# MLP up-projection of column groups 2 to 7 as Strassen 2x2 block products

## Chip, cores and metric

One core of one Trainium2 chip. The metric is the device time of one execution in microseconds (us); the kernel before takes 691.36 us, the median of three runs (689.93 to 691.77).

## What is computed

Two decoder layers on x of 256 rows by 1024 columns in float32: layer 0 is retention, layer 1 MoBA attention, each followed by a squared-ReLU MLP. What matters here is the MLP, twice:

```
h = relu(x @ w_up)          # [256, 1024] @ [1024, 4096]
y = (h * h) @ w_down        # [256, 4096] @ [4096, 1024]
```

## The kernel before

Every float32 product is made of three float32r matmuls on two parts of each operand: hi*hi, hi*lo and lo*hi (`mm`, lines 176 to 181). The activations are held transposed in two parts (class `HT`: `hi` and `lo`, eight k tiles of 128 by 256 rows). Rows come in two row tiles t of 128, the 4096 hidden columns in eight groups g of 512.

**The weight stream.** Class `Stream` (lines 90 to 160) brings all weights in chunks of 128 x 1024 in the order of use. `load` issues one chunk's DMA on the SP queue into one of four `raw` buffers; `split` makes its two parts: ScalarE copies it, rounded, into `whi` (line 134), and VectorE takes the difference into `wlo` (line 135). Ten pairs of parts can be live. `get` hands the next chunk to a product; if none is split yet, it splits one at that place in the program. An up-projection chunk is two k tiles of one group of 512 columns; a down-projection chunk is one k tile of 1024 columns.

**What sets the order.** There is no scheduler at run time: each engine carries out its instructions in the order in which the Python code emits them. Class `Flow` keeps a model time `now` that the matmuls advance. After each product step `advance` lets side chains (generators that yield a delay) go on, and calls `pump`, which emits a split when a slot is free and `next_t` has been reached. After a split, `next_t` is moved on by 1.3 or 2.0 model us.

**The MLP** (`mlp`, from line 396). Groups 0 and 1 are computed by `in_groups_skewed` with the activations stationary; `act_rows` squares them and transposes them on TensorE. For each group g from 2 to 7, `up_cols` takes four chunks and makes the transposed result at once, weights stationary: four 128-column tiles, eight k tiles, three matmuls of 256 columns each, into two PSUM tiles `upc`. `act_cols` then runs Relu on ScalarE (line 417), the square on VectorE (line 419) and the split into the parts of `hid[g]` (lines 197 and 198). Behind each group four k steps of the down projection follow (`step_out`; hidden group g-2), each twelve matmuls of 512 columns into `dn`. In the last layer the second half of row tile 1's accumulator is two tiles of 256 columns (line 452). The last eight k steps are done by `finish_out` or `finish_last`.

Of the kernel before, what the change touches and what calls it, by code (L numbers as in the profile page):

```python
# [17 lines left out]
P = 128  # L18
# [66 lines left out]
class Chunk:  # L85
    def __init__(self, hi, lo):
        self.hi, self.lo, self.left = hi, lo, CH * S


class Stream:  # L90
    """Weight chunks in the order of use: loaded, then split into two float32r parts."""

    def __init__(self, tc, ctx, flow, slots, raws):
# [3 lines left out]
        self.src, self.raw, self.ready = [], [], []  # L97
        self.live, self.next_t, self.dma_t = 0, 0.0, 0.0
        flow.pump = self.pump

    def load(self):
        """issue the next chunk's load, and the other loads that come before it"""
        while self.src:
            s = self.src.pop(0)
            self.dma_t = max(self.dma_t, self.flow.now + 1.6)
            if callable(s):
                s()
                self.dma_t += 1.0
                continue
# [10 lines left out]
            return  # L120

    def split(self, pres=(None,)):
        nc = self.nc
        if not self.raw:
            self.load()
        raw = self.raw.pop(0)[0]
# [10 lines left out]
        self.ready.append(Chunk(hi, lo))  # L137
        self.next_t = max(self.next_t, self.flow.now) + (1.3 if len(self.ready) < 4 else 2.0)
        while len(self.raw) < self.raws and self.src:
            self.load()  # L140

    def pump(self):
        while self.live < self.slots and self.flow.now >= self.next_t:
            if not self.raw:
                self.load()
            if not self.raw or self.flow.now < self.raw[0][1]:
                return
            self.split()
# [14 lines left out]
def body(ctx, tc, xT, x, gT, gpost, w_in_0, w_out_0, w_up_0, w_down_0, w_in_1, w_out_1, w_up_1, w_down_1,  # L163
# [12 lines left out]
    def mm(o, a, b, first, last):  # L176
        """o += a.T @ b; a, b: (hi, lo) pairs of float32r parts."""
        nc.tensor.matmul(o, a[0], b[0], start=first, stop=False)  # L178
        nc.tensor.matmul(o, a[0], b[1], start=False, stop=False)  # L179
        nc.tensor.matmul(o, a[1], b[0], start=False, stop=last)  # L180
        flow.now += 3 * b[0].shape[-1] / 2400
# [766 lines left out]
```

## Time and profile before

| | |
|---|---|
| runs, median (lowest to highest) | 691.36 us (689.93 to 691.77) |
| profiled execution, span from first to last instruction | 688.4 us |
| its own time outside the span | not listed; the runs' median is 3.0 us above the span |
| TensorE matmuls (PE) busy | 676.1 us, 98% |
| VectorE (DVE) busy | 419.4 us, 61% |
| ScalarE (ACT) busy | 350.4 us, 51% |
| DMA | 125.09 MB, 182 GB/s in the mean |

Busy time of PE is the time covered by matmuls, whose ends are modelled and overlap the next one's start. So the pace of TensorE is read from the distance between two starts, not from the duration of one. For DVE and ACT both exist: the duration of one instruction, which counts where another engine waits for its end, and the distance between two starts on the same engine, which counts in an unbroken sequence. A releaser ("<-") is what ended an idle time.

### The profile page before, as it was taken

How to read it: one execution, taken by the hardware profiler on the slowest of the kernel's cores; microseconds unless marked ns; L12 is line 12 of the kernel's file. 1: busy time of each engine (PE TensorE's matmuls, PEld its weight loads, DVE VectorE, ACT ScalarE, POOL GpSimd, SP SyncE). 2: the span in 40 equal slices, each digit the busy share in tenths (PEclk: the TensorE clock that was granted, in tenths of full speed). 3: DMA queues.
4: the chain of work that ended last, by engine and by line, in shares of the span. 5: the costliest groups of instructions: out<-in, count | busy, mean ns of one | idle time of the engine just before them, and what ended most of it. 6: DMA issues, size and time to landing. Idle time of an engine off the chain costs nothing. (4 is left out here: it accounts for less than half of the span.)

```text
span 688.4 us, 10014 instructions
## 1 busy us (share of the span) xinstructions
PE 676.1 (98%) x3919; PEld 594.3 (86%) x3919; DVE 419.4 (61%) x521; ACT 350.4 (51%) x493; POOL 82.2 (12%) x138
## 2 busy tenths in 40 slices
PE   8999999999999999999999999999999999999996
PEld 6889898988888988998898878888889999999985
DVE  5669576656458665545653867867686654465513
ACT  6475555445346545435542657755465554345411
POOL 0222120201001000000000263922010000000001
PEclk9999999999999999999999999999999999999998
DMA  7767565464624774457545456543246744674401
GB/s 274 284 208 267 200 212 177 155 206 154 241 93 157 241 251 169 157 190 244 176 140 175 169 184 219 184 148 123 83 161 235 258 155 151 211 231 148 164 9 62
DMA packets 36191, 125.09 MB, mean 182 GB/s; under 512 B 4272, under 2 KB 4784, under 8 KB 36144
## 3 DMA queue, kind: packets, MB, share of 16 engines
q1 hardware_dynamic: 36144, 124.45, 53.0%
q8 instruction: 31, 0.51, 0.3%
q14 instruction: 16, 0.13, 0.1%
HBM read 123.39 MB, written 1.05 MB: 181 GB/s over the span
## 5 line engine op out<-in xcount | busy, mean ns | idle before, releaser
L135 DVE TENSOR_TENSOR wlo<-raw,whi 128x1024 fp32r<-128x1024 f32 (+1 forms) x227 | 271.5, 1212 | 114.1 <-ACT whi L134 112.8
L134 ACT ACTIVATE whi<-raw 128x1024 fp32r<-128x1024 f32 (+1 forms) x227 | 231.1, 1042 | 86.9 <-DMA raw<-in_w_down 21.1
L178 PE MATMUL ip<-whi,act 128*128 128x512 f32 x288 | 114.2, 397 | 0.0
L179 PE MATMUL ip<-wlo,act 128*128 128x512 f32 x288 | 112.5, 391 | 0.2 <-DVE wlo L135 0.2
L180 PE MATMUL ip<-whi,act 128*128 128x512 f32 x288 | 112.4, 390 | 0.0
L178 PE MATMUL upc<-act,whi 128*128 128x256 f32 x384 | 108.8, 283 | 0.0
L180 PE MATMUL upc<-act,wlo 128*128 128x256 f32 x384 | 108.7, 283 | 0.0
L179 PE MATMUL upc<-act,whi 128*128 128x256 f32 x384 | 108.7, 283 | 0.0
L179 PE MATMUL dn<-wlo,act 128*128 128x512 f32 (+1 forms) x288 | 105.6, 367 | 0.0
L178 PE MATMUL dn<-whi,act 128*128 128x512 f32 (+1 forms) x288 | 105.6, 367 | 0.0
L180 PE MATMUL dn<-whi,act 128*128 128x512 f32 (+1 forms) x288 | 105.3, 366 | 0.0
L178 PEld LDWEIGHTS upc<-act,whi 128*128 128x128 f32 x384 | 73.7, 192 | 0.3
L179 PEld LDWEIGHTS upc<-act,whi 128*128 128x128 f32 x384 | 73.7, 192 | 0.3
L180 PEld LDWEIGHTS upc<-act,wlo 128*128 128x128 f32 x384 | 73.7, 192 | 0.0
L180 PEld LDWEIGHTS ip<-whi,act 128*128 128x128 f32 x288 | 54.1, 188 | 11.6
L179 PEld LDWEIGHTS ip<-wlo,act 128*128 128x128 f32 x288 | 54.2, 188 | 10.7 <-DVE wlo L135 0.7
L178 PEld LDWEIGHTS ip<-whi,act 128*128 128x128 f32 x288 | 54.2, 188 | 10.0
L178 PEld LDWEIGHTS dn<-whi,act 128*128 128x128 f32 x288 | 54.4, 189 | 8.9
L180 PEld LDWEIGHTS dn<-whi,act 128*128 128x128 f32 x288 | 54.2, 188 | 8.9
L179 PEld LDWEIGHTS dn<-wlo,act 128*128 128x128 f32 x288 | 54.4, 189 | 8.6
L310 POOL TENSOR_TENSOR po_c<-po_sum,mhalf 128x1 f32<-128x1 f32 x8 | 4.5, 563 | 379.4 <-DVE po_sum L298 379.4
L417 ACT ACTIVATE r<-upc 128x512 f32<-128x512 f32 x24 | 14.3, 597 | 60.8 <-PE upc L180 60.8
(156 smaller groups left out, 862.4 us busy)
## 6 DMA issues: line engine op xcount, KB each, us to landing
raw<-in_w_in SPq DMA_DIRECT2D x69, 512.0 KB, 3.9
raw<-in_w_up SPq DMA_DIRECT2D x64, 512.0 KB, 4.5
raw<-in_w_down SPq DMA_DIRECT2D x64, 512.0 KB, 4.1
raw<-in_w_out SPq DMA_DIRECT2D x24, 512.0 KB, 3.3
gb<-in_gpost SPq DMA_DIRECT2D x4, 512.0 KB, 5.4
raw<-in_w_in SPq DMA_DIRECT2D x6, 256.0 KB, 5.6
h<-in_x SPq DMA_DIRECT2D x2, 512.0 KB, 6.6
dT_sb<-in_dT SPq DMA_DIRECT2D x4, 256.0 KB, 4.8
```

The source lines that it names most:

```text
L134: nc.scalar.activation(hi[:, c], raw[:, c], AF.Copy)
L135: nc.vector.tensor_sub(lo[:, c], raw[:, c], hi[:, c].bitcast(F32))
L178: nc.tensor.matmul(o, a[0], b[0], start=first, stop=False)
L179: nc.tensor.matmul(o, a[0], b[1], start=False, stop=False)
L180: nc.tensor.matmul(o, a[1], b[0], start=False, stop=last)
L310: nc.gpsimd.tensor_tensor(c, self.ss, mhalf, ALU.pow)
L417: nc.scalar.activation(r, o, AF.Relu)
```

## The change

Groups 2 to 7 are taken in three blocks of two groups (g, g+1). A block's product is a 2x2 block product: the activations in quarters by row tile and by even and odd k tiles, the weights in quarters by even and odd k tiles and by group (`_blocks` on the host reorders `w_up` accordingly). Seven products of quarters, Winograd's form of Strassen's scheme, take the place of eight. `product` makes one: four k tiles, three matmuls each, activations stationary, 512 columns, two chunks of weights.

The activation sums (`hsum`) are made once per MLP by `block_sums`. Four of the seven products of a block need sums of weight quarters: the quarters are loaded into four tiles `quad` (128 x 2 x 1024), and `Stream.split` adds one to another in place on VectorE before it splits the sum. The results are put together from PSUM by VectorE (`u2`, `u3`, `c`); Relu and the square run on ScalarE (`squared`); as the result is not transposed now, `turned` transposes it on TensorE and splits it. `down()` is one k step of the down projection; eight of them stand between and behind a block's products. `pump` waits also for the model's landing time of the quarters, and a split costs 1.3 to 2.3 model us. The last layer's accumulator is no longer divided into 256 columns.

```diff
+    def loaded(self):
+        op = self.order[0]
+        if op is None:
+            return self.raw[0][1] if self.raw else None
+        t = [self.landed.get(n) for n in op.needs]
+        return None if None in t else max(t)
...
+        while self.loaded() is None:
+            assert self.load()
+        op = self.order.pop(0)
         hi = self.pool.tile([P, CH], F32R, tag="whi", name="whi", bufs=self.slots)
         lo = self.pool.tile([P, CH], F32R, tag="wlo", name="wlo", bufs=self.slots)
+        full = len(self.ready) >= 4
+        if op is None:
+            raw = self.raw.pop(0)[0]
+            cost = 2.0 if full else 1.3
+        else:
+            raw = self.quads[op.q][:, op.half, :]
+            cost = 1.7 if full else 1.3
+            if op.add is not None:
+                nc.vector.tensor_add(raw, raw, self.quads[op.add][:, op.half, :])
+                cost += 0.6 if full else 1.0
...
             nc.scalar.activation(hi[:, c], raw[:, c], AF.Copy)
             nc.vector.tensor_sub(lo[:, c], raw[:, c], hi[:, c].bitcast(F32))
         self.live += 1
-        self.ready.append(Chunk(hi, lo))
-        self.next_t = max(self.next_t, self.flow.now) + (1.3 if len(self.ready) < 4 else 2.0)
-        while len(self.raw) < self.raws and self.src:
-            self.load()
+        self.quad_ops += op is not None
+        self.ready.append(Chunk(hi, lo, CH * S if op is None else CH * P))
+        self.next_t = max(self.next_t, self.flow.now) + cost
+        while len(self.raw) < self.raws and self.load():
+            pass
...
-        def act_cols(g, jp, o):
-            r = new_e2([P, 2, S], "r")
-            nc.scalar.activation(r, o, AF.Relu)
-            sq = new_e2([P, 2, S], "sq")
-            nc.vector.tensor_mul(sq, r, r)
+        def turned(g, t, c):
+            yield 1.6
+            tp = new_ps([P, 4, P], "tp_u")
+            turn4(tp, c)
+            ts = slice(t * P, (t + 1) * P)
+            split(hid[g][:, 0, :, ts], hid[g][:, 1, :, ts], tp)
+        def squared(g, t, o, add=None, sign=1.0):
+            c = new_e2([P, 512], "c")
+            if add is None:
+                nc.scalar.activation(c, o, AF.Relu, scale=sign)
+            else:
+                nc.vector.tensor_add(c, o, add)
+                nc.scalar.activation(c, c, AF.Relu, scale=sign)
+            nc.scalar.activation(c, c, AF.Square)
+            done[g].append(flow.spawn(turned(g, t, c)))
+        s_hi, s_lo = [p.tile([P, 4, 4, P], F32R, name=n, tag="act" if p is act else n)
+                      for p, n in ((act, "s_hi"), (qpool, "s_lo"))]
+        def block_sums():
+            (a11, a12), (a21, a22) = [[hg[:, t, e::2, :] for e in range(2)] for t in range(NT)]
+            f = [new_e2([P, 4, P], "hsum") for _ in range(4)]
+            nc.vector.tensor_sub(f[0], a22, a21)
             yield 0.8
+            nc.vector.scalar_tensor_tensor(f[1], f[0], -1.0, a11, op0=ALU.mult, op1=ALU.subtract)
+            split(s_hi[:, 0], s_lo[:, 0], f[0])
+            yield 1.6
+            nc.vector.tensor_sub(f[2], a11, a21)
+            split(s_hi[:, 1], s_lo[:, 1], f[1])
+            yield 1.6
+            nc.vector.scalar_tensor_tensor(f[3], f[1], -1.0, a12, op0=ALU.mult, op1=ALU.subtract)
+            split(s_hi[:, 2], s_lo[:, 2], f[2])
+            yield 1.6
+            split(s_hi[:, 3], s_lo[:, 3], f[3])
...
-        def up_cols(g):
-            chunks = [ws.get() for _ in range(4)]
-            for jp in range(2):
-                o = new_ps([P, 2, S], "upc")
-                for j in range(2):
-                    f0 = (jp * 2 + j) * P
-                    for k in range(KD):
-                        s = slice((k % 2) * 512 + f0, (k % 2) * 512 + f0 + P)
-                        mm_cols(o[:, j, :], chunks[k // 2], s, hT.both(k), k == 0, k == KD - 1)
-                done[g].append(flow.spawn(act_cols(g, jp, o)))
+        def quad(t, e):
+            return lambda kp: hT.tile(2 * kp + e, t)
+        def hsum(i):
+            return lambda kp: (s_hi[:, i, kp, :], s_lo[:, i, kp, :])
+        def product(o, lhsT, first):
+            for half in range(2):
+                w = ws.get()
+                for kk in range(2):
+                    kp = 2 * half + kk
+                    mm_rows(o, lhsT(kp), w, slice(kk * 512, (kk + 1) * 512), first and kp == 0, kp == 3,
+                            not first)
+        def up_blocks(g, down):
+            x = new_ps([P, 512], "px")
+            product(x, quad(0, 0), True)
+            p1 = new_e2([P, 512], "p1")
+            nc.scalar.activation(p1, x, AF.Copy)
+            down()
+            z = new_ps([P, 512], "pz")
+            product(z, hsum(0), True)
+            down()
+            y = new_ps([P, 512], "py")
+            product(y, hsum(1), True)
+            u2 = new_e2([P, 512], "u2")
+            nc.vector.tensor_add(u2, y, p1)
+            down()
+            product(y, hsum(2), False)
+            u3 = new_e2([P, 512], "u3")
+            nc.vector.tensor_add(u3, y, p1)
+            squared(g + 1, 1, z, u3, -1.0)
+            down()
+            product(x, quad(0, 1), False)
+            squared(g, 0, x)
+            down()
+            product(y, quad(1, 1), False)
+            squared(g, 1, y, p1)
+            down()
+            product(z, hsum(3), False)
+            squared(g + 1, 0, z, u2, -1.0)
+            down()
+            down()
...
+        sums = flow.spawn(block_sums())
-        if nxt is None:
-            acc[1] = [acc[1][0], acc[1][1][:, :256], new_ps([P, 256], "dn4")]
         nk = FF // P
-        for g in range(2, NG):
+        ks = iter(range(nk - SKEW))
+        def down():
+            k, w = next(ks), ws.get()
+            for t in range(NT):
+                step_out(acc, lhs, k, t, w, nk)
+        for g in range(2, NG, 2):
+            new_hid(g + 1)
             new_hid(g)
-            up_cols(g)
-            for k in range((g - 2) * 4, (g - 1) * 4):
-                w = ws.get()
-                for t in range(NT):
-                    step_out(acc, lhs, k, t, w, nk)
+            flow.finish(sums)
+            up_blocks(g, down)
+        ws.quads = None
...
+            gates = (0, 0, 0, 0) if b == 0 else (last + 8, last + 12, last + 12, last + 14)
+            at = (8 * b - 1, 8 * b + 1, 8 * b + 1, 8 * b + 2) if b else (0, 0, 0, 1)
+            for i in range(4):
+                for half in range(2):
+                    q = QuadLoad(place[i], half, up[c0 + 2 * i + half], gates[i], (b, i, half))
+                    due.setdefault(at[i], []).append(q)
+            q1, q2, q3, q4 = place
+            ops = [(q1, None, (0,)), (q1, q2, (0, 1)), (q1, q3, (0, 2)), (q2, q3, (1, 2)), (q4, None, (3,)),
+                   (q1, q4, (0, 3)), (q3, None, (2,))]
+            for j, (q, add, needs) in enumerate(ops):
+                ws.order += [QuadOp(q, add, half, [(b, i, half) for i in needs]) for half in range(2)]
+                ws.order += [None] * (1 if j < 6 else 2)
+            place = [q2, q4, q1, q3]
```

Here is VectorE's queue in block 2 of the first MLP (groups 4 and 5), and the corresponding place before (group 4). `raw` is a chunk of `w_down`, `quad0` to `quad3` are the weight quarters, `py`, `pz` and `px` the products in PSUM, `tp_u` the transposed squares, `act` is `hid`. Before:

```order
L135 TENSOR_TENSOR wlo_2711<-raw_2631,whi_2710 128x1024
L135 TENSOR_TENSOR wlo_2738<-raw_2649,whi_2737 128x1024
L419 TENSOR_TENSOR sq_2748<-r_2746 128x512
L198 TENSOR_TENSOR act_2678<-sq_2748,act_2678 128x512
L135 TENSOR_TENSOR wlo_2784<-raw_2667,whi_2783 128x1024
L419 TENSOR_TENSOR sq_2809<-r_2807 128x512
L135 TENSOR_TENSOR wlo_2815<-raw_2687,whi_2814 128x1024
L198 TENSOR_TENSOR act_2678<-sq_2809,act_2678 128x512
```

Now:

```order
L177 TENSOR_TENSOR quad1_2030<-quad1_2030,quad0_2029 128x1024
L185 TENSOR_TENSOR wlo_2703<-quad1_2030,whi_2702 128x1024
L535 TENSOR_TENSOR u2_2713<-py_2695,p1_2640 128x512
L185 TENSOR_TENSOR wlo_2716<-raw_2557,whi_2715 128x1024
L177 TENSOR_TENSOR quad3_2032<-quad3_2032,quad0_2029 128x1024
L185 TENSOR_TENSOR wlo_2734<-quad3_2032,whi_2733 128x1024
L177 TENSOR_TENSOR quad3_2032<-quad3_2032,quad0_2029 128x1024
L185 TENSOR_TENSOR wlo_2745<-quad3_2032,whi_2744 128x1024
L539 TENSOR_TENSOR u3_2755<-py_2695,p1_2640 128x512
L481 TENSOR_TENSOR c_2757<-pz_2659,u3_2755 128x512
L185 TENSOR_TENSOR wlo_2762<-raw_2576,whi_2761 128x1024
L250 TENSOR_TENSOR act_2614<-tp_u_2778,act_2614 128x4x128
```

A sum and its difference now stand next to each other; u2 reads the product whose last chunk is split in the row just ahead of it; the next chunk's split stands behind u2. The row on `tp_u` reads the transposed form of the `c` two rows above it.

ScalarE's queue at the same place. Before:

```order
L134 ACTIVATE whi_2737<-raw_2649 128x1024
L417 ACTIVATE r_2746<-upc_2679 128x512
L197 ACTIVATE act_2678<-sq_2748 128x512
L134 ACTIVATE whi_2783<-raw_2667 128x1024
L417 ACTIVATE r_2807<-upc_2750 128x512
```

Now:

```order
L184 ACTIVATE whi_2744<-quad3_2032 128x1024
L482 ACTIVATE c_2757<-c_2757 128x512
L483 ACTIVATE c_2757<-c_2757 128x512
L184 ACTIVATE whi_2761<-raw_2576 128x1024
L249 ACTIVATE act_2614<-tp_u_2778 128x4x128
L184 ACTIVATE whi_2788<-quad2_2031 128x1024
L184 ACTIVATE whi_2798<-quad2_2031 128x1024
L479 ACTIVATE c_2808<-px_2616 128x512
L483 ACTIVATE c_2808<-c_2808 128x512
L184 ACTIVATE whi_2811<-raw_2624 128x1024
```

The next down chunk (`whi_2761`, later `whi_2811`) stands behind the Relu and the square of the product just ended.

TensorE's queue behind u3, where that down chunk is used. Before, behind an up-projection group, the `dn` matmuls followed without a transposition:

```order
L180 MATMUL upc_2750<-act_1667,wlo_2608 128x256
L178 MATMUL dn_2252<-whi_2627,act_2256 128x512
L179 MATMUL dn_2252<-wlo_2628,act_2256 128x512
L180 MATMUL dn_2252<-whi_2627,act_2256 128x512
L178 MATMUL dn_2253<-whi_2627,act_2256 128x512
```

Now:

```order
L230 MATMUL dn_2261<-whi_2761,act_2264 128x512
L231 MATMUL dn_2261<-wlo_2762,act_2264 128x512
L232 MATMUL dn_2261<-whi_2761,act_2264 128x512
L254 MATMUL tp_u_2778<-ident_96,c_2757 128x128 x4
L230 MATMUL dn_2262<-whi_2761,act_2264 128x512
L231 MATMUL dn_2262<-wlo_2762,act_2264 128x512
L232 MATMUL dn_2262<-whi_2761,act_2264 128x512
L230 MATMUL px_2616<-whi_2788,act_1668 128x512
```

The four transpositions of `c` stand behind nine of the twelve `dn` matmuls of the chunk `whi_2761`.

## Rows read from the trace of the kernel before

**Rows 1.** Busy time by engine, whole span.

```profile
PE 676.1 (98%) x3919; PEld 594.3 (86%) x3919; DVE 419.4 (61%) x521; ACT 350.4 (51%) x493; POOL 82.2 (12%) x138
```

**Rows 2.** Windows: two middle groups; groups 2 to 7. Stretch, length; busy PE, PEld, DVE, ACT, POOL; clock; DMA.

```profile
275.30:320.20 44.90, 44.90 (x290) 41.11 (x289) 24.58 (x25) 20.88 (x24) 0.00 (x0) 1.00 0.57 187
230.40:365.20 134.80, 134.80 (x869) 123.48 (x868) 77.21 (x78) 65.52 (x77) 0.00 (x0) 1.00 0.60 197
```

**Rows 3.** Timeline of PE, group 2's up and down projection; start, duration.

```profile
230.39 0.28 PE L178 MATMUL upc<-act,whi 128*128 128x256 f32 x1
230.50 0.28 PE L179 MATMUL upc<-act,whi 128*128 128x256 f32 x1
230.62 0.28 PE L180 MATMUL upc<-act,wlo 128*128 128x256 f32 x1
...
242.34 0.40 PE L178 MATMUL dn<-whi,act 128*128 128x512 f32 x1
242.57 0.40 PE L179 MATMUL dn<-wlo,act 128*128 128x512 f32 x1
...
253.25 0.28 PE L178 MATMUL upc<-act,whi 128*128 128x256 f32 x1
```

**Rows 4.** Timeline of PE, one transposition of four tiles in group 1.

```profile
228.56 0.60 PE L202 MATMUL tp_u<-ident,sq 128*128 128x128 f32 x4
228.91 0.48 PE L178 MATMUL ip<-whi,act 128*128 128x512 f32 x1
229.23 0.39 PE L179 MATMUL ip<-wlo,act 128*128 128x512 f32 x1
```

**Rows 5.** Groups of instructions by form, DVE and ACT: count, busy us, mean ns, idle before.

```profile
L135 DVE TENSOR_TENSOR wlo<-raw,whi 128x1024 fp32r<-128x1024 f32 x221 | 267.6, 1226 | 113.4 <-ACT whi L134 112.1
L134 ACT ACTIVATE whi<-raw 128x1024 fp32r<-128x1024 f32 x221 | 227.6, 1054 | 86.5 <-DMA raw<-in_w_down 21.1 <-PE upc L179 15.4 <-DMA raw<-in_w_up 15.4
L417 ACT ACTIVATE r<-upc 128x512 f32<-128x512 f32 x24 | 14.3, 597 | 60.8 <-PE upc L180 60.8
L197 ACT ACTIVATE act<-sq 128x512 fp32r<-128x512 f32 x24 | 15.0, 624 | 10.4 <-DVE sq L419 10.4
L198 DVE TENSOR_TENSOR act<-tp_u,act 128x512 fp32r<-128x512 f32 x8 | 5.5, 690 | 8.7 <-ACT act L197 8.5
L197 ACT ACTIVATE act<-tp_u 128x512 fp32r<-128x512 f32 x8 | 4.8, 599 | 16.5 <-PE tp_u L202 16.5
```

**Rows 6.** Timeline of DVE: an unbroken sequence at the end of the first out projection.

```profile
202.45 1.22 DVE L135 TENSOR_TENSOR wlo<-raw,whi 128x1024 fp32r<-128x1024 f32 x1
203.59 1.29 DVE L198 TENSOR_TENSOR act<-hg,act 128x512 fp32r<-128x512 f32 x2
204.79 1.22 DVE L135 TENSOR_TENSOR wlo<-raw,whi 128x1024 fp32r<-128x1024 f32 x1
```

**Rows 7.** Timeline of ACT behind the last `upc` matmul of group 2.

```profile
242.60 0.60 ACT L417 ACTIVATE r<-upc 128x512 f32<-128x512 f32 x1 [1.28 <-PE upc L180]
243.09 1.05 ACT L134 ACTIVATE whi<-raw 128x1024 fp32r<-128x1024 f32 x1
244.04 0.61 ACT L197 ACTIVATE act<-sq 128x512 fp32r<-128x512 f32 x1
```

**Rows 8.** Timeline: the last `upc` matmul of group 2, then a handover chain in group 3.

```profile
242.22 0.28 PE L180 MATMUL upc<-act,wlo 128*128 128x256 f32 x1
...
259.20 0.60 ACT L417 ACTIVATE r<-upc 128x512 f32<-128x512 f32 x1 [4.58 <-PE upc L180]
259.83 0.69 DVE L419 TENSOR_TENSOR sq<-r 128x512 f32<-128x512 f32 x1 [3.95 <-ACT r L417]
260.55 0.63 ACT L197 ACTIVATE act<-sq 128x512 fp32r<-128x512 f32 x1 [0.76 <-DVE sq L419]
```

**Rows 9.** Windows at the kernel's start; columns as in rows 2, granted clock third from the right.

```profile
5.50:8.90 3.40, 2.08 (x10) 1.47 (x11) 1.87 (x3) 1.68 (x4) 0.00 (x0) 1.00 0.96 327
8.90:12.30 3.40, 3.40 (x19) 3.40 (x18) 3.37 (x7) 3.36 (x7) 0.00 (x0) 0.51 1.05 395
12.30:15.70 3.40, 3.40 (x30) 3.40 (x30) 2.12 (x5) 2.22 (x5) 0.00 (x0) 0.99 1.02 407
```

**Rows 10.** The waits of PE over the whole span, longest first: us, times, longest.

```profile
PE tp_q L202 <- POOL yq L719: 2.2, 2, 1.6
PE qk L178 <- ACT whi L134: 1.2, 2, 0.9
```

More of the change, by code (lines that the diff above doesn't have):

```diff
@@ L96, in __init__, with add, open_quads @@
         self.flow, self.slots, self.raws = flow, slots, raws
-        self.src, self.raw, self.ready = [], [], []
+        self.src, self.order, self.raw, self.ready = [], [], [], []
+        self.quads, self.landed, self.quad_ops = None, {}, 0
         self.live, self.next_t, self.dma_t = 0, 0.0, 0.0
         flow.pump = self.pump
+    def add(self, *loads):
+        self.src += loads
+        self.order += [None for s in loads if not callable(s)]
+    def open_quads(self, tiles):
+        self.quads, self.landed = tiles, {}
     def load(self):
         while self.src:
-            s = self.src.pop(0)
+            s = self.src[0]
+            if isinstance(s, QuadLoad) and (self.quads is None or s.gate > self.quad_ops):
+                return False
+            self.src.pop(0)
             self.dma_t = max(self.dma_t, self.flow.now + 1.6)
+            if isinstance(s, QuadLoad):
+                self.nc.sync.dma_start(self.quads[s.q][:, s.half, :], s.src)
+                self.dma_t += 1.46
+                self.landed[s.name] = self.dma_t + 0.9
+                continue
             if callable(s):
@@ L136, in split @@
         self.live += 1
[L137 to L146 removed]
+        self.quad_ops += op is not None
[3 more added lines that the diff above has]
+            pass
+    def pump(self):
+        while self.order and self.live < self.slots and self.flow.now >= self.next_t:
+            while self.loaded() is None:
+                if not self.load():
+                    return
+            if self.flow.now < self.loaded():
                 return
@@ L173, in body, with mm, mm_rows @@
     ws = Stream(tc, ctx, flow, 10, 4)
[L176 to L180, printed above, removed]
+    def mm(o, a, b, first, last, again=False):
+        nc.tensor.matmul(o, a[0], b[0], start=first, stop=False, skip_group_check=again)
+        nc.tensor.matmul(o, a[0], b[1], start=False, stop=False, skip_group_check=again)
+        nc.tensor.matmul(o, a[1], b[0], start=False, stop=last, skip_group_check=again)
         flow.now += 3 * b[0].shape[-1] / 2400
-    def mm_rows(o, a, w, s, first, last):
-        mm(o, a, (w.hi[:, s], w.lo[:, s]), first, last)
+    def mm_rows(o, a, w, s, first, last, again=False):
+        mm(o, a, (w.hi[:, s], w.lo[:, s]), first, last, again)
         n = s.stop - s.start
@@ L393, in in_groups_skewed, with mlp @@
             then(g, 1, o)
-    def mlp(hT, gain, nxt, gi):
+    def mlp(hT, gain, nxt, gi, qpool):
+        ws.open_quads([qpool.tile([P, 2, CH], F32, name=f"quad{i}") for i in range(4)])
         hid = [None] * NG
@@ L536, in body, with add_mlp @@
-    src += mlp_order(w_up_0, w_down_0)
-    src += [w_in_1[g * 4 + c] for g in (0, 1, 3, 4, 2, 5) for c in range(4)]
-    src += [w_out_1[k] for k in range(MH)]
-    src += mlp_order(w_up_1, w_down_1)
+            ws.add(lambda: consts.update(gb=load_gain(0)))
+    ws.add(*[w_out_0[k] for k in range(16)])
+    def add_mlp(up, down, base):
+        ws.add(*[up[c] for c in range(8)])
+        place = [0, 1, 2, 3]
+        due = {}
+        nb = (NG - 2) // 2
+        for b in range(nb):
+            c0 = 8 + 8 * b
+            last = base + 14 * (b - 1)
+            gates = (0, 0, 0, 0) if b == 0 else (last + 8, last + 12, last + 12, last + 14)
[11 more added lines that the diff above has]
+            place = [q2, q4, q1, q3]
+        ws.order += [None] * 8
+        for k in range(FF // P):
+            ws.src += due.get(k, []) + [down[k]]
@@ L541, in start_k @@
+    add_mlp(w_up_0, w_down_0, 0)
+    ws.add(*[w_in_1[g * 4 + c] for g in (0, 1, 3, 4, 2, 5) for c in range(4)])
+    ws.add(*[w_out_1[k] for k in range(MH)])
+    add_mlp(w_up_1, w_down_1, 14 * ((NG - 2) // 2))
     def start_k(k):
@@ L883, in _groups, with _blocks @@
     return w.reshape(n * 4, P, CH)
+def _blocks(w):
+    c = [_groups(w, np.arange(1024))]
+    for b in range(1, w.shape[1] // 1024):
+        v = w[:, b * 1024:(b + 1) * 1024].reshape(2, 2, 2, P, 2, 512)
+        for e, g in ((0, 0), (0, 1), (1, 1), (1, 0)):
+            c.append(v[:, :, e, :, g, :].transpose(0, 2, 1, 3).reshape(2, P, CH))
+    return np.concatenate(c)
 def _constants():
```

49 lines of the change are left out of this document (22 added, 27 removed).

## Prediction

> **What bounds the kernel now.** I read the busy times first. TensorE is covered for 98% of the span, VectorE for 61% [rows 1]. The windows say the same of the stretch that changes: over groups 2 to 7 of the first MLP TensorE has no gap in 134.8 us, and two middle groups with their eight down steps take 44.9 us, in which VectorE is busy 24.6 us and ScalarE 20.9 [rows 2]. The list of waits confirms it: the longest single wait of TensorE in the whole span is 1.6 us, and none lies in an MLP [rows 10]. So time is won here only by shortening TensorE's queue, and only as long as the other two engines keep ahead of it.
>
> TensorE's pace comes from the starts. From 230.39 to 242.34 stand 96 up-projection matmuls of 256 columns and one group of transpositions; from 242.34 to 253.25 stand 48 matmuls of 512 [rows 3], so one costs 10.91/48 = 0.227 us. Four transpositions and a 512-column matmul take 0.67 us, hence four transpositions 0.44 [rows 4]. The 256-column matmul is then (11.95 - 0.44)/96 = 0.120 us, just over half of the 512-column one; little is won by the wider form itself.
>
> **What the change does to TensorE.** Per block of two groups 192 matmuls of 256 columns (23.0 us) go, and 7 x 12 = 84 of 512 columns come (19.1 us). Four groups of transpositions are added (1.8 us). With 96 down matmuls (21.8 us) a block is 42.7 us of TensorE work against 44.9: a gain of 2.2 us a block, 13 us over six blocks, if nothing waits. The undivided accumulator of the last layer wins 96 x (2 x 0.120 - 0.227) = 1.2 us and makes the last part of the tail twice as wide, which is of the same size; I cost both together at nothing.
>
> **What it does to VectorE and ScalarE.** A block has 14 chunks of quarters and 8 down chunks to split, 8 sums, 5 additions from PSUM and 4 splits behind transpositions. In an unbroken sequence the distance between starts is 1.14 us for 1024 columns (202.45 to 203.59) and 0.60 for 512 [rows 6]. The sum of quarters has no row of its own; its nearest row is the difference of the same size, 1226 ns long [rows 5], and I take that. Bounds: the 512-column form from below, 0.6 us; no row suggests more than 1.4. VectorE: 30 x 1.14 + 9 x 0.60 = **39.6 us** a block. ScalarE: 22 copies at 0.95 (243.09 to 244.04) and 13 of 512 columns at about 0.5 (242.60 to 243.09) [rows 7], 27 us. Both fit under 42.7 us; the count of work alone does not make this slower.
>
> **The waits do.** The printed queues show what a count hides: in block 2 no chunk is split ahead of its use. u2 reads the product of the chunk split one row above it, and the next split comes after u2. So each engine waits for the other in turn. A handover costs the full duration of the earlier instruction plus 0.03 us between ScalarE and VectorE (259.20 + 0.60 to 259.83; 259.83 + 0.69 to 260.55) and about 0.1 behind TensorE (242.22 + 0.28 [rows 8] to 242.60 [rows 7]). Exposed idle time of VectorE, per block:
>
> - A sum and its difference stand together, and between them ScalarE must copy the sum: 1.23 + 0.03 + 1.05 + 0.03, less the 1.14 already counted, is 1.2 us; eight times, 9.6 us.
> - u2, u3 and two of the `c` wait for the end of a product whose last chunk was just split: five matmuls and the handovers, 1.5 us; four times, 6.0.
> - The following down chunk's copy stands on ScalarE behind Relu and square (0.6 us each [rows 5]), and its difference behind that: 0.69 + 0.63 + 0.53 + 1.05 + 0.09 - 0.60 = 2.4 us, three times; for the product `px`, which has no row on VectorE in between, its end is waited for too, 4.0. Together 11.2.
> - The split behind the transposition waits for nine down matmuls, the transposition, and ScalarE's copy of it: 1.23 + 0.03 + 8 x 0.227 + 0.60 + 0.1 + 0.60 + 0.03 - 1.14 = 3.3 us; four times, 13.0.
> - Smaller ones: the copy `p1` ahead of a sum's copy (1.4), chunks behind a transposition (three of 0.35), 2.5 in all.
>
> That is 42.3 us of waiting on top of 39.6: **82 us** for block 2, and the same for block 3. Block 1 starts with six chunks and two sums split ahead. Behind its first product VectorE still has 22 instructions of 1024 columns (25.1 us), the eight of the activation sums, two left from group 1 and nine of 512 columns (together 11.4); it waits behind six sums (7.2), four transpositions, about 2.4 each as the next chunk is split already (9.6), one down chunk (2.4) and the activation sums (1.3): 57 us. An MLP's six groups take 57 + 82 + 82 = 221 us instead of 134.8: 86 us more, and **172 us** for the two layers, whose queues read alike.
>
> ScalarE and VectorE may not pass a waiting row: in the rows VectorE stands idle 3.95 us before a square whose Relu is late [rows 8], though that alone does not prove the order. The Trainium skill, page "TensorE: Matmul & The Clock Gate", section "Architectural detail: the array is 16× 32×32, not 1× 128×128", says that these two engines take their queues strictly first in, first out; by that rule nothing softens the sum above, and no run here shows it alone.
>
> **TensorE's clock.** At the kernel's start TensorE issued ten matmuls in 3.4 us, waiting between them for splits. In the following 3.4 us the granted clock was 0.51, that is the lower level, 1.2 GHz, although it was busy throughout: 19 matmuls instead of the 30 of the next stretch [rows 9]. In blocks 2 and 3 TensorE works 42.7 of 82 us, in bursts with pauses up to 3.9 us, so this can return. Bounds: nothing, or the lower level throughout, which doubles the matmuls that VectorE waits for: 1.1 us for each of five product ends, 2.4 for each of four transpositions and 1.4 for the first product, 16 us a block, half of that in block 1, so 40 us a layer. The start's row resembles these blocks, but its stretch was poorer in matmuls than their mean; I take half, 20 us a layer, **40 us**.
>
> The Trainium skill, the same page, section "HAM oscillation — how this bites in real kernels", tells of a kernel whose matmuls come in bursts between waits and whose clock falls again before every burst. By that rule the sum would be the third rival's below. The first window [rows 9] agrees with it; no MLP row here can.
>
> DMA stays hidden: the same bytes, the engines' share 0.60 over the stretch [rows 2], and now spread over a longer one. POOL does nothing there.
>
> Sum: span 688.4 + 172 + 40 = 900 us. The runs' median lies 3.0 us above the span, so **903 us**.
>
> **Rivals.**
>
> 1. *Faster.* The waits are covered: splits stay enough ahead, TensorE sets the pace, and the 13 us are won: 691.4 - 13 = 678 us. The place is the queue of VectorE in blocks 2 and 3; it decides at 42.7 - 39.6 = 3.1 us of exposed wait a block for the full gain and at 44.9 - 39.6 = 5.3 for no change. For it: the work fits, and block 1 does have a lead. Against it: the queue's order, which alone puts 9.6 us between sums and differences. Chance 0.05, of which 0.01 for no change.
> 2. *Only the sums' handover shows.* The waits for products and transpositions overlap with splits after all: 39.6 + 9.6 = 49.2 us a block, 3 x 49.2 - 134.8 = 13 us a layer, 717 us; with some of the other waits anything up to 840. Chance 0.12.
> 3. *The lower clock nearly throughout:* 688.4 + 172 + 80 + 3 = 943 us. Chance 0.16.
> 4. *The clock stays up:* 688.4 + 172 + 3 = 863 us. Chance 0.25.
>
> That the change does less than it says is no rival: TensorE's queue holds 504 matmuls of the products against 1152 of `upc`, 7/8 of the columns.
>
> **How the numbers follow.** The forecast, waits as added up and the clock down for part of the time, has 0.42. Cases 3 and 4 lie inside the range, with 0.83 in all. Its lower end, 840, is case 4 with block times 5% shorter (11 us a layer); its upper end, 945, is case 3. Below 840 lie rivals 1 and 2. A measurement of this kernel can tell 0.3% from no change; faster 0.04, within 0.3% 0.01, slower 0.95.
>
> **What would show it.** In the profile after, TensorE's busy share over the blocks falls to about half; VectorE idles before `wlo` behind `whi` and before `act` behind `tp_u`; the distance from u2 to u2 of the next block is 80 us or more; each sum is followed by a difference 2.3 us later. The granted clock there tells cases 3 and 4 apart. The prediction is wrong if `whi` of a down chunk starts before the square ahead of it, or if blocks 2 and 3 take under 60 us.

## The result and the profile after

The changed kernel takes **909.9 us** (median of four runs, 908.0 to 910.7), the kernel before beside it 690.9. The ratio is 1.316, with a 95% interval of 1.314 to 1.319. The forecast was 903 us, the range 840 to 945. The profiled execution has a span of 905.9 us, so 217.5 us more than before.

Busy time by engine, whole span, answers to [rows 1]:

```profile
PE 752.4 (83%) x3271; PEld 585.3 (65%) x3271; DVE 530.4 (59%) x624; ACT 408.2 (45%) x565; POOL 79.1 (9%) x138
```

TensorE issues 648 matmul records less than before and is covered for 83% of the span in place of 98%. VectorE has 111 us more work than before, but its 530 us would fit even into the span before. Work alone does not explain 217 us; the engines must be waiting.

The windows of the three blocks of the first MLP, each from the first matmul of `px` to that of the next block, the third to the end of its down steps (columns as in [rows 2]):

```profile
230.68:289.40 58.72, 47.55 (x202) 36.43 (x200) 42.84 (x46) 31.39 (x41) 0.00 (x0) 0.94 0.42 144
289.40:381.56 92.16, 62.85 (x198) 42.74 (x196) 42.25 (x41) 29.58 (x35) 0.00 (x0) 0.80 0.27 91
381.56:473.80 92.24, 62.91 (x199) 42.62 (x198) 42.07 (x40) 29.59 (x35) 0.00 (x0) 0.81 0.14 47
```

Together 243.1 us against 134.8 for the same groups before [rows 2], 108.3 us more. In the second layer the three take 242.9 us, against about 136 before. That is some 215 us of the loss of 217.5. The DMA share falls to 0.27 and 0.14 where before it was 0.57, and no wait of VectorE or ScalarE in block 2 ends with a transfer: transfers bound nothing here. The granted clock, third from the right, is 0.80 where it was 1.00.

VectorE's timeline in block 2 (start, duration, engine, line, operation; in brackets the idle time before it and what ended it):

```profile
302.25 1.22 DVE L177 TENSOR_TENSOR quad<-quad,quad 128x1024 f32<-128x1024 f32 x1
304.60 1.23 DVE L185 TENSOR_TENSOR wlo<-quad,whi 128x1024 fp32r<-128x1024 f32 x1 [1.12 <-ACT whi L184]
307.36 0.69 DVE L535 TENSOR_TENSOR u<-py,p 128x512 f32<-128x512 f32 x1 [1.54 <-PE py L232]
...
350.93 0.69 DVE L481 TENSOR_TENSOR c<-py,p 128x512 f32<-128x512 f32 x1 [2.59 <-PE py L232]
353.92 1.23 DVE L185 TENSOR_TENSOR wlo<-raw,whi 128x1024 fp32r<-128x1024 f32 x1 [2.30 <-ACT whi L184]
360.50 0.69 DVE L250 TENSOR_TENSOR act<-tp_u,act 128x512 fp32r<-128x512 f32 x1 [5.36 <-ACT act L249]
```

Each of the large kinds of wait that the prediction summed is there in turn: a difference 2.35 us behind its sum's start; u2 behind the end of `py`; the down chunk's difference 2.30 us late, since its copy stood behind Relu and square; the split behind the transposition 5.36 us late. The last one is longer than forecast (3.3), and TensorE's timeline of the same stretch shows why:

```profile
355.20 0.80 PE L231 MATMUL dn<-wlo,act 128*128 128x512 f32 x1 [0.47 <-DVE wlo L185]
355.79 0.63 PE L232 MATMUL dn<-whi,act 128*128 128x512 f32 x1
356.22 0.63 PE L230 MATMUL dn<-whi,act 128*128 128x512 f32 x1
...
358.78 1.05 PE L254 MATMUL tp_u<-ident,c 128*128 128x128 f32 x4
359.49 0.65 PE L230 MATMUL dn<-whi,act 128*128 128x512 f32 x1
```

The matmuls behind the pause start 0.43 us apart, not 0.227 [rows 3]: the lower level, 1.2 GHz (from 354.0 to 359.4 the granted clock is 0.50). Eight of them cost 1.6 us more and the transpositions some 0.4, which takes 3.3 to 5.3.

### The profile page after: what moved, and what is told of

The parts are those of the page before. It is cut to its first block, busy times and chain, and to the rows that moved or that the text cites. A ratio compares the mean times of both kernels' runs of the same rounds, so it can differ in the third digit from the quotient of the medians.

```text
span 905.9 us, 8789 instructions
## 1 busy us (share of the span) xinstructions
PE 752.4 (83%) x3271; PEld 585.3 (65%) x3271; DVE 530.4 (59%) x624; ACT 408.2 (45%) x565; POOL 79.1 (9%) x138
## 4 chain that ended last, share of the span: by engine, by line
PE 48%; DVE 24%; ACT 16%; issue 5%; POOL 3%; DMA 3%; SPq 0%; DVEq 0%; POOLq 0%; ACTq 0%
DVE wlo L185 14%; ACT whi L184 10%; DVE quad L177 6%; PE ip L231 5%; PE ip L232 5%; PE ip L230 5%; PE dn L231 3%; PE dn L232 2%; PE out L232 2%; PE out L230 2%; PE out L231 2%; PE tp_u L254 2%; PE qk L232 2%; PE qk L230 2%; PE qk L231 2%
## 5 line engine op out<-in xcount | busy, mean ns | idle before, releaser
L185 DVE TENSOR_TENSOR wlo<-raw,whi 128x1024 fp32r<-128x1024 f32 (+1 forms) x179 | 213.9, 1209 | 112.1 <-ACT whi L184 110.9
L184 ACT ACTIVATE whi<-raw 128x1024 fp32r<-128x1024 f32 (+1 forms) x179 | 181.7, 1036 | 34.6 <-PE out L232 10.9
L230 PE MATMUL dn<-whi,act 128*128 128x512 f32 x256 | 118.9, 464 | 50.8 <-ACT whi L184 50.8
L184 ACT ACTIVATE whi<-quad 128x1024 fp32r<-128x1024 f32 x84 | 87.1, 1054 | 117.4 <-DVE quad L177 117.4
L185 DVE TENSOR_TENSOR wlo<-quad,whi 128x1024 fp32r<-128x1024 f32 x84 | 101.6, 1223 | 60.0 <-ACT whi L184 60.0
L231 PE MATMUL dn<-wlo,act 128*128 128x512 f32 x256 | 117.1, 458 | 20.0 <-DVE wlo L185 19.9
L232 PE MATMUL dn<-whi,act 128*128 128x512 f32 x256 | 112.1, 438 | 0.0
L250 DVE TENSOR_TENSOR act<-tp_u,act 128x512 fp32r<-128x512 f32 x32 | 22.1, 689 | 94.9 <-ACT act L249 94.9
L249 ACT ACTIVATE act<-tp_u 128x512 fp32r<-128x512 f32 x32 | 19.0, 594 | 101.0 <-PE tp_u L254 101.0
L177 DVE TENSOR_TENSOR quad<-quad,quad 128x1024 f32<-128x1024 f32 x48 | 58.5, 1218 | 0.0
L230 PE MATMUL qk<-act,whi 128*128 128x256 f32 x128 | 37.3, 292 | 1.3 <-ACT whi L184 1.3
```

Source lines behind the costliest of these rows:

```text
L177: nc.vector.tensor_add(raw, raw, self.quads[op.add][:, op.half, :])
L184: nc.scalar.activation(hi[:, c], raw[:, c], AF.Copy)
L185: nc.vector.tensor_sub(lo[:, c], raw[:, c], hi[:, c].bitcast(F32))
L230: nc.tensor.matmul(o, a[0], b[0], start=first, stop=False, skip_group_check=again)
L231: nc.tensor.matmul(o, a[0], b[1], start=False, stop=False, skip_group_check=again)
L232: nc.tensor.matmul(o, a[1], b[0], start=False, stop=last, skip_group_check=again)
```

## The experiments

A block is 42.7 us of TensorE work. The table gives the medians; block 2 is the stretch between two first `px` matmuls as above. Each stands beside runs of the kernel before on the same chip, whose median was 689.9 to 691.3 us. e2_pairs, e4_nosums, e5_fill, e8_late and e11_vector_squares ran once, the others four times. Four runs of one kernel lie up to 6 us apart, so the 10 and 11 us that e11_vector_squares and e5_fill win as a whole are less certain than the large differences.

| kernel | median us | block 2, us | its clock |
|---|---|---|---|
| changed | 909.9 | 92.2 | 0.80 |
| e5_fill | 898.8 | 85.8 | 0.90 |
| e11_vector_squares | 899.8 | 87.8 | 0.83 |
| e8_late | 887.2 | 85.4 | 0.84 |
| e2_pairs | 864.0 | 83.5 | 0.84 |
| e4_nosums | 853.1 | 79.8 | 0.85 |
| e1_lead | 848.5 | 68.2 | 0.87 |
| e3_lead_pairs | 800.3 | 61.5 | 0.89 |
| e6_lead_pairs_late | 737.3 | 51.2 | 0.97 |
| e7_paced | 735.5 | 50.7 | 0.93 |
| e12_early_sums | 728.1 | 49.4 | 0.97 |
| e9_pool_sums | 753.6 | 51.4 | 0.93 |
| e10_pool_sums_start | 757.7 | 51.7 | 0.93 |

The theory is that of the prediction: VectorE's order, in which every chunk is split just ahead of its use, makes the engines wait in turn. The rivals are that VectorE's added work bounds it whatever the order, and, for single terms, that a wait taken away only moves.

### The lead given back

```diff
-        self.next_t = max(self.next_t, self.flow.now) + cost
+        self.next_t = self.flow.now if self.quads else max(self.next_t, self.flow.now) + cost
```

> The work is the same; only the time from which the next chunk may be split is no longer pushed on by each split, so that inside the MLPs the splits run ahead as far as the ten pairs of whi and wlo allow. Theory A (the lost lead: what is added to the time is waiting, because each chunk is split just before its use): VectorE's work of about 40 to 43 us a block and TensorE's 42.7 lie beside each other again, blocks 2 and 3 take 45 to 55 us instead of 92, the granted clock goes back to 0.95 or more, and the time is 690 to 740 us. Theory B (the added work on VectorE itself, or the dependence of products on squares and transpositions, is the bound whatever the order): blocks stay above 80 us and the time above 870.

848.5 us, ratio 1.232 (1.228 to 1.236), block 2 at 68 us: both lie between the two theories' ranges. The same work in another order is 61 us faster, so the order costs time, and theory B's "whatever the order" falls. But a new wait took the place of the old ones, and block 1, which already had a lead, got longer, 84.8 us in place of 58.7. The two largest waits of TensorE follow (us, times, longest); in the kernel before TensorE waited at most 1.6 us [rows 10]:

```profile
PE tp_u L254 <- ACT c L483: 80.0, 24, 6.7
PE tp_u L254 <- DVE sq L460: 30.6, 4, 13.2
```

`turned` queues the transposition 1.6 us of TensorE's work behind the square. With splits queued ahead, the square is late by more than that, and now TensorE stands. The second line is the squares of groups 0 and 1, which stand behind splits and activation sums at the start of block 1.

### Single waits of the changed kernel

Without the weight sums, so that the products are formed with unsummed quarters:

```diff
-                nc.vector.tensor_add(raw, raw, self.quads[op.add][:, op.half, :])
```

> The additions of weight quarters (eight a block) are left out, so the products are formed with unsummed quarters; all else is as in the changed kernel. Theory A (the waits add up in turn, and a sum costs its own 1.23 us and 1.2 us of handover to ScalarE): 2.4 x 8 = 19 us a block in blocks 2 and 3, some 14 in block 1, 105 us over both layers: about 800 us, and blocks 2 and 3 at 73 us. Theory C (the sums lie beside other waits, a product or a transposition is late anyway): less than 50 us won, 860 or more.

853.1 us: 57 us less, half of what theory A gave and just over theory C's 50. Block 2 loses 12.4 us of 19. Its VectorE rows show where the rest went:

```profile
297.70 0.69 DVE L534 TENSOR_TENSOR u<-py,p 128x512 f32<-128x512 f32 x1 [4.67 <-PE py L231]
...
305.17 0.69 DVE L538 TENSOR_TENSOR u<-py,p 128x512 f32<-128x512 f32 x1 [3.37 <-PE py L231]
```

u2 and u3 now wait 8.0 us in place of 3.1: VectorE reaches them sooner, the product that they read ends no sooner. In block 1, which has a lead, the sums' absence won only 5 us (6.6 in the second layer).

Both halves of a sum added ahead of both splits:

```diff
+            if op.add is not None and op.half == 0:
+                for i in range(2):
+                    z = self.quads[op.q][:, i, :]
+                    nc.vector.tensor_add(z, z, self.quads[op.add][:, i, :])
```

> The changed kernel with the two halves of a weight sum added one after the other ahead of both splits; no lead is given back. Theory A (each of the eight sums a block costs a handover of 1.2 us, of which half is saved when two additions stand together and ScalarE copies the first sum under the second): 4 x 2.4 = 9.6 us less a block in blocks 2 and 3, up to 55 us in all, about 855 us. Theory F (a wait that is taken away only lengthens the next one, as leaving out the sums altogether won 57 us where 105 were expected): 0 to 25 us, 885 us or more.

864.0 us, 46 us less; block 2 8.6 us shorter, 9.6 expected. VectorE's waits for copies of quarters in block 2 fall from 9.6 us to 0.7. Nearly all of that price comes back, and the time is near theory A's 855: the handover is a cost on the path.

The transpositions later, in `turned`:

```diff
-            yield 1.6
+            yield 6.0
```

> The changed kernel with one number changed: the four transpositions of a squared tile are put into TensorE's queue 6.0 us of its work behind the square, not 1.6. The work and the lead of the splits stay as they are. Theory G (the wait of VectorE ahead of the split behind a transposition, 3.3 us expected and 4.6 to 5.4 measured, four times a block, is time on the path, and is a matter of where the transposition stands): those waits fall below 2 us, blocks 2 and 3 take 78 to 84 us instead of 92, the time is 850 to 880 us. Theory A in its strict form (without lead every product still waits for its own split, so the wait only moves): 895 to 915.

887.2 us, block 2 at 85.4: between the two theories. The four waits behind the transposition fall from 20.2 to 11.9 us, but the difference of the down chunk behind `px` now waits 6.99 us (3.96 before): with no split behind a transposition ahead of it, VectorE meets the whole length of `px` there. The wait moved in part.

The squares of the blocks on VectorE:

```diff
-            nc.scalar.activation(c, c, AF.Square)
+            nc.vector.tensor_mul(c, c, c)
```

> The changed kernel with the squares of the blocks on VectorE (a multiplication of 128x512) instead of ScalarE; nothing else. Theory A: the copy of the next down chunk no longer stands behind the square on ScalarE (0.66 us less in three waits a block), but VectorE gets 4 x 0.6 us of work and must itself wait for Relu ahead of it (about 0.7 us each): 2 to 4 us more a block at the most, 905 to 935 us. Theory J (the copies behind the squares are a large part of the loss, 11 us a block as summed): 6 us or more a block less, under 880.

899.8 us, 10 us *less*: neither theory. The down chunk's waits in block 2 go from 11.1 to 1.3 us, while VectorE's waits for Relu add 4.4 and four squares about 2.4. That is some 3 us won. The block is 4.4 us shorter, as the last two products' ends also wait 2.6 us less, their matmuls 0.23 us apart here. Block 3 and the second layer's blocks 2 and 3 are 3.1, 0.6 and 1.9 us shorter. The expectation had the added work right and the saving too small; the square on ScalarE is at most a small loss in this order.

### TensorE's clock

Twelve matmuls of 512 columns ahead of each transposition, into the tile that it overwrites:

```diff
-            yield 1.6
             tp = new_ps([P, 4, P], "tp_u")
+            for i in range(12):
+                nc.tensor.matmul(tp, hT.hi[:, 0, :P], hT.hi[:, 0:2, :], start=True, stop=True)
+            yield 1.6
```

> Twelve matmuls of 512 columns, whose results are overwritten by the transposition behind them, stand ahead of each group of four transpositions in the blocks; they use operands that are long there. TensorE gets 48 x 0.227 = 11 us more work a block, in the pause in which it waits for Relu and square. Theory D (the waits that came out longer than worked out, 4.6 to 5.4 us ahead of the split behind a transposition instead of 3.3, come from the lower clock after pauses): the granted clock of blocks 2 and 3 rises from 0.80 to 0.95 or more and the blocks get shorter in spite of the added work, 80 to 88 us instead of 92, the time 860 to 895 us. Theory E (they are late for a reason other than the clock): the added matmuls lengthen the blocks or leave them, 92 to 103 us, the time 905 to 970.

898.8 us in all. The window of block 2 (columns as above):

```profile
294.31:380.09 85.78, 66.94 (x246) 47.68 (x244) 42.79 (x41) 29.85 (x36) 0.00 (x0) 0.90 0.28 98
```

48 more matmuls, 11 us more TensorE work, and the block is 6.4 us *shorter*. That is theory D, though the clock stays under its 0.95 and the whole time just over its 895. The clock rises from 0.80 to 0.90 and the four waits behind the transposition are 4.64, 3.29, 3.28 and 3.27 us, three of them the 3.3 of the prediction's sum. In block 3 and in the second layer's blocks 2 and 3 these waits sum to 13.1 us a block, the forecast's 13.0, and the block is 3.2 to 4.7 us shorter; the waits for products' ends stay there at 9.0 to 10.0. Block 1, whose TensorE has few pauses to fill, gets 5 us longer, which is why the whole wins only 11 us.

### How far the order carries

The edits of e1_lead and e2_pairs together:

> As e1_lead, and the two halves of a weight sum are added one after the other before the first of them is copied, so that ScalarE's copy of one half lies under the addition of the other. Theory A: the waits between sum and copy go as well, blocks at 43 to 50 us, 675 to 715 us in all. If the handover between sum and copy costs nothing once there is a lead, the time is that of e1_lead within 5 us. Theory B: above 870, as in e1_lead.

800.3 us, ratio 1.160 (1.158 to 1.161), none of the three expected times; once more TensorE's wait for the square is the largest that is left, 59.2 us in 24 places. One of them is a pause of 2.62 us; about 1 us behind its end matmuls start 0.43 us apart:

```profile
296.42 0.39 PE L235 MATMUL dn<-whi,act 128*128 128x512 f32 x1
299.44 0.66 PE L257 MATMUL tp_u<-ident,c 128*128 128x128 f32 x4 [2.62 <-ACT c L486]
...
300.66 0.63 PE L233 MATMUL dn<-whi,act 128*128 128x512 f32 x1
301.09 0.63 PE L234 MATMUL dn<-wlo,act 128*128 128x512 f32 x1
```

Then e8_late's edit (`yield 6.0`) on top:

> As e3_lead_pairs, and the transpositions stand 6.0 us behind the square, as in e8_late. In e3_lead_pairs TensorE waited 59 us in 24 places for the squared tile ahead of a transposition, and ran at the lower clock behind several of these pauses. Theory A: with lead, paired sums and late transpositions TensorE's queue has no wait left in the blocks but those around the start of block 1 (10.7 us there in e3_lead_pairs): blocks 2 and 3 at 43 to 48 us and the time 700 to 735 us. Theory B (VectorE's work with its unavoidable handovers is the bound): blocks stay above 55 us, 770 us or more.

737.3 us, ratio 1.066 (1.063 to 1.069), just over theory A's span, and its blocks 2 and 3 at 51 us, not 43 to 48: with a lead, the late transposition is worth 63 us, without it 23. Next, a pace for the lead:

```diff
-        self.next_t = self.flow.now if self.quads else max(self.next_t, self.flow.now) + cost
+        self.next_t = (max(self.next_t, self.flow.now - 3.0) + (1.15 if op is None or op.add is None or op.half else 2.8)
+                       if self.quads else max(self.next_t, self.flow.now) + cost)
```

> As e6_lead_pairs_late, with the lead given at a pace: each split moves the time of the next one on by 1.15 us, a pair of sums by 2.8, and up to 3 us of it may be caught up, instead of splitting whatever fits at once. So the squares of groups 0 and 1 no longer stand behind a row of splits at the start of block 1. Theory A: another 5 to 10 us a layer, 680 to 715 us; if VectorE's 40 us a block against TensorE's 42.7 leave too little to hold the lead, 715 to 760. It beats the kernel before (690) only if the blocks come to less than 45 us each.

735.5 us, no further than e6 and in the range given for a VectorE that cannot hold the lead. In its block 2 VectorE is busy 41.1 of 50.7 us:

```profile
288.36:339.02 50.66, 46.29 (x197) 37.25 (x196) 41.11 (x40) 29.66 (x36) 0.00 (x0) 0.93 0.47 166
```

So the sums were moved to POOL, each as soon as its quarters are there (a pair of sums then no longer moves the pace on by 2.8):

```diff
-                    nc.vector.tensor_add(z, z, self.quads[op.add][:, i, :])
+            self.nc.gpsimd.tensor_add(z, z, self.quads[o.add][:, o.half, :])
```

> As e7_paced, but the sums of weight quarters are made on POOL, which does nothing in the MLPs, each as soon as the last reader of the old contents is queued and its quarters are loaded; so up to a product ahead of its split. In e7_paced VectorE was busy 41.1 of a block's 50.7 us and late by 8 us at the last square of a block. Theory H (VectorE's load is what is left of the loss): 8 x 1.14 = 9.1 us of it go, TensorE's 42.7 us set the block again, 44 to 47 us, and the time is 695 to 712 us. Rival I (POOL's sum, for which the nearest row is 0.87 to 0.99 us for 256 columns, 3.5 to 4 us if it goes by columns, is too slow for the chain of sums in one quarter, or VectorE's instructions get longer beside it): 735 us or more.

and, with `yield 8.0` for `yield 3.0` in `act_rows` as well:

> As e9_pool_sums, and the transpositions of groups 0 and 1, which end just ahead of the first block, stand 8.0 us of TensorE's queue behind their square and not 3.0. In e7_paced TensorE waited 10.7 us in each layer for the last of these squares, which stood behind splits and activation sums. Theory H: up to 10 us a layer on top of e9_pool_sums, 678 to 695 us, at or under the 691 of the kernel before. If the pause only moves to the next product's operands (the activation sums stand in the same queue): within 5 us of e9_pool_sums.

753.6 and 757.7 us: rival I by the time, and the later transpositions won nothing. POOL's sum takes 2.95 us, less than expected, but VectorE's differences get longer; groups by form of e9_pool_sums:

```profile
L208 POOL TENSOR_TENSOR quad<-quad,quad 128x1024 f32<-128x1024 f32 x48 | 140.7, 2948 | 150.6 <-DVE wlo L185 141.6 <-DMA quad<-in_w_up 8.0
L185 DVE TENSOR_TENSOR wlo<-quad,whi 128x1024 fp32r<-128x1024 f32 x84 | 121.9, 1466 | 37.3 <-ACT whi L184 36.3
```

The loss lies where the two overlap: the first `px` starts at 238.9, 8 us later than in e7_paced, and block 1 takes 64.6 us (57.7 there). Block 3 is another matter, since POOL made almost all of its sums during block 2:

```profile
354.86:398.67 43.81, 43.24 (x197) 35.20 (x196) 32.91 (x31) 29.39 (x36) 4.75 (x3) 1.00 0.44 146
```

With 32.9 us of work VectorE keeps ahead, TensorE waits 0.6 us in all, and the block takes 43.8 us (43.4 in e10_pool_sums_start) against 44.9 in the kernel before [rows 2]. There theory H holds, and the product wins 1.1 to 1.5 of its 2.2 us a block.

Last, on top of e7_paced, VectorE's pair of sums one down chunk ahead of its splits, and all transpositions 8.0 us behind their square (`yield 8.0` in `turned` and `act_rows`):

```diff
+            if self.quads and self.order and self.order[0] and self.loaded():
+                self.sum(self.order[0])
```

`sum` holds the two additions of e2_pairs and makes them once.

> As e7_paced, but a pair of sums is queued on VectorE one down chunk ahead of its splits, so that ScalarE copies that chunk under the additions and finds the sums ready; and all transpositions in and ahead of the blocks stand 8.0 us behind their square. Theory H (VectorE's load, 41 us a block and 48 in block 1, plus its remaining waits now sets the pace): blocks 2 and 3 at 44 to 48 us, block 1 at 50 to 54, 705 to 725 us, not below 691, as VectorE's work alone, 130 us a layer, leaves too little. If TensorE's 42.7 us set it: 680 to 695.

728.1 us, ratio 1.053 (1.051 to 1.055), 182 us under the changed kernel and the best of the study, just over theory H's range and not below the kernel before. Its three blocks:

```profile
231.20:286.14 54.94, 46.63 (x202) 37.27 (x200) 46.47 (x49) 31.78 (x39) 0.00 (x0) 0.91 0.46 163
286.14:335.51 49.37, 44.57 (x197) 36.23 (x196) 40.02 (x40) 29.31 (x35) 0.00 (x0) 0.97 0.48 171
335.51:385.00 49.49, 44.72 (x194) 36.26 (x193) 37.53 (x38) 29.08 (x35) 0.00 (x0) 0.93 0.41 135
```

153.8 us a layer against 134.8: the 38 us that are left. TensorE's waits behind them, in blocks 1 and 2:

```profile
243.86 0.80 PE L240 MATMUL dn<-whi,act 128*128 128x512 f32 x1 [7.94 <-ACT act L259]
...
308.11 0.77 PE L240 MATMUL py<-whi,s_hi 128*128 128x512 f32 x1 [4.10 <-DVE u L545]
```

The first waits for ScalarE's copy of a tile that TensorE had transposed at 233.93. The copy (243.22) stands behind those of the activation sums, for which ScalarE idles 5.16 us, as VectorE comes to them (237.35) only behind sums and splits. The second writes `py` anew, which u2 must read first, and u2 (307.28, the product ended by 301.2) stands behind a pair of sums and four splits. VectorE's work, 38 to 46 us a block, is about as long as TensorE's 42.7, so where it runs ahead with splits it is late for these; block 3 of e9_pool_sums, with 32.9, is not. Whether a second bank for the third product, or u2 queued sooner, wins the 4.1 us was not tried.

## Why the prediction was right

**Point by point, for block 2.** VectorE's waits there sum to 49.9 us, 42.3 forecast:

| term | forecast | changed kernel | e5_fill |
|---|---|---|---|
| sums to differences | 9.6 | 9.1 | 9.1 |
| ends of products (u2, u3, two `c`) | 6.0 | 9.0 | 7.7 |
| down chunks behind Relu and square | 11.2 | 10.9 | 10.9 |
| splits behind transpositions | 13.0 | 20.2 | 14.5 |
| small ones | 2.5 | 0.8 | 0.8 |
| sum | 42.3 | 49.9 | 43.0 |

- *TensorE's work.* An unbroken stretch of e3_lead_pairs (304.96 to 321.06) has 71 distances of 0.227 us. 42.7 us a block stands; of the gain of 2.2 us a block, 1.1 to 1.5 were reached only in block 3 of the two kernels with sums on POOL.
- *VectorE's work*, 39.6 forecast, is 92.2 - 49.9 = 42.3 us. The count is right, the size a little low: an instruction followed by a wait, as 23 are here, costs its 1.23 us, not the 1.14 between starts in an unbroken sequence. This is one of the places that put 909.9 above 903.
- *The waits* came out term by term within half a microsecond, all but the two that hold matmuls and the small ones, of which the 1.4 us of `p1` shows in block 3 (10.6 us between sums and differences) and not in block 2.
- *The clock*, for which half of 40 us a layer was taken, is most of what those two have over the forecast: 3.0 and 7.2 us in block 2, where half the bound had been 8. For the transpositions e5_fill shows it: with TensorE kept busy their waits fall to 14.5 us in block 2 and to 13.1 in the three other such blocks. That half of the bound came so close was a choice that came out, not a working: the prediction had no row that gave the share. For the products' ends the same wait stands in the trace at both levels. In block 2 `c` waits 2.59 us (350.93) behind matmuls 0.43 us apart; in the second layer's block 2 it waits 1.52, the forecast's 1.5, behind matmuls 0.23 us apart:

```profile
754.36 0.69 DVE L481 TENSOR_TENSOR c<-py,p 128x512 f32<-128x512 f32 x1 [1.52 <-PE py L232]
```

- *Rival 3*, the lower level nearly throughout, gave 943 us; measured are 909.9, with the granted clock at a mean of 0.80 in these blocks and matmuls at both paces. The Trainium skill, page "TensorE: Matmul & The Clock Gate", section "HAM oscillation — how this bites in real kernels", tells of a kernel whose clock falls again ahead of every burst. The trace agrees with that in part: behind the pause of 3.77 us ahead of 321.54 matmuls start 0.43 us apart where they had been 0.23 apart in front of it, but behind the one of 1.69 us ahead of 309.24 they stay 0.23 apart.
- *Block 1*: 57 forecast, 58.7 measured, but in part by luck. VectorE's work there is 42.1 us, not 36.5, as 26 instructions of 1024 columns fall into the block, not 22; the waits are 16.6, not 20.5, as only two of the four transpositions are waited for (5.5 us, not 9.6). The two errors nearly cancel. Blocks 2 and 3: 82 and a share of the 20, 92.2 each.
- *Signs named:* from u2 to u2 93.0 us (307.36 to 400.40), a difference 2.35 us behind its sum, the copy of the down chunk behind the square (352.31, 352.85). TensorE's busy share in block 2 is 68% by covered time, over the half forecast, since lower-clock matmuls cover more; by its work it is 42.7 of 92.2.

**The rivals.** 1 and 2 fell: in blocks 2 and 3 the waits stand one behind the other and make up the block's length. e2_pairs shows the term on which rival 2 built, the sums' handover, as a cost of 46 us, no more. 4 (863) fell with the clock at 0.80. Rival 1's condition, splits ahead, can be made (e1_lead and those built on it), but even there TensorE waits for VectorE and 678 is not reached.

**What the sum does not tell** is what one wait is worth alone: without the sums 105 us were expected and 57 came, as the next product's end took over. The terms of a chain add up to the time, but what one term would win alone can be less.

## What to carry to other kernels

Before work is moved to an engine with room, look at where its instructions stand: here TensorE's and VectorE's work were both near 42.5 us a block and the block took 92, because each split stood just ahead of its use. Most of that can be had back by order alone (910 to 728 us), but a saving of 5% on the busiest engine is gone when a second engine is then as full: in the one block where VectorE had 33 us and not 38 to 42, part of the saving was there. A producer that runs ahead makes others late that stand behind it in the same queue (TensorE's 80 us of waits for squares in e1_lead): every later stage's place in its queue has to be moved along with the first one's.

## What the hardware showed besides

**POOL beside VectorE.** A difference of 1024 columns takes 1.22 us on the mean in the changed kernel. In e9_pool_sums, while POOL runs six sums from 280.96 to 299.01, two of them take:

```profile
283.00 2.37 DVE L185 TENSOR_TENSOR wlo<-raw,whi 128x1024 fp32r<-128x1024 f32 x1 [0.25 <-ACT whi L184]
285.41 3.30 DVE L185 TENSOR_TENSOR wlo<-quad,whi 128x1024 fp32r<-128x1024 f32 x1
```

The Trainium skill, page "SBUF — State Buffer", section "Who interferes with whom", says that a VectorE instruction with two SBUF inputs contends with a GpSimd instruction that reads SBUF. The rows agree: both engines' instructions have two SBUF inputs, and the two differences are 1.2 and 2.1 us longer. An idle POOL is not free for work of this form. e9_pool_sums changed the order and the pace as well, so how much of its 18 us over e7_paced is contention alone is open.

**A kernel can be faster with more matmuls.** e5_fill's block 2 does 11 us more on TensorE in 6.4 us less, since the matmuls and transpositions that VectorE's splits wait for then run at the higher level (waits of 3.3 us in place of 5.4). Where TensorE had few pauses, in block 1, the same matmuls cost 5 us.
